# Splitting a convolution chunk between accumulating DMAs and VectorE, and preparing projection weights two tiles ahead, in a two-layer conv / attention / expert trunk

## The chip, the cores and the metric

The kernel runs on one core of one Trainium2 chip. The metric is the device time of one execution in microseconds (us); the median of the runs is given. The core's engines work side by side, each through its own queue in program order: TensorE (PE, matmuls; its weight loads are listed as PEld), VectorE (DVE), ScalarE (ACT), GpSimd (POOL) and SyncE (SP). DMAs are issued from the SP, ACT and POOL queues.

## The reference, cut to what matters

Two layers, each a mixer block and then an expert lookup, over 16 meta tokens and 256 tokens of width 1024. The change lies in the mixer:

```python
h = _rmsnorm(x, mix_g); z = h @ w_in          # conv_in, c_q, c_kv, k_rope, gate_logits
u = conv_in[..., :512] * sigmoid(conv_in[..., 512:])
u = _causal_depthwise_conv(u, conv_w, conv_b)  # 31 taps for each of 512 channels
u = silu(_layernorm(u, conv_ln_g, conv_ln_b)); y_conv = u @ w_conv_out
q = (_rmsnorm(c_q, q_a_g) @ w_uq); kv = (_rmsnorm(c_kv, kv_a_g) @ w_ukv)   # 8 heads
y_mla = chunk_causal_attention(q, k, v) @ w_mla_out
gates = sigmoid(gate_logits)
merged = gates[..., :1024] * y_conv + gates[..., 1024:] * y_mla
x = x + merged @ w_out
```

Then `_peer` picks 128 of 16384 experts for each token, and adds their outputs to `x`.

## The kernel before, in words

Everything is float32, channels on the 128 partitions and the T = 272 tokens along the free dimension (layer 1 computes only the last 256 in most places). The order of the instructions on each engine is written out by hand: Python generators (`attention`, `conv2`, `layernorm`) are advanced a step at a time between the matmul tiles, and whatever a step issues goes to the queues there.

**Weights.** `next_w` hands out weight tiles of 128 x 1024 from a ring of four 1 MB buffers `wraw`, which SP loads (line 85); `peek_w(n)` looks n tiles ahead.

**The gate loop.** `ztile` makes one 128-channel tile of `z` by eight matmuls. After eight tiles for the conv input (`upad`, four chunks of 128 channels) come 16 gate tiles, `for i in range(16)`. In each, DVE scales the tile (`g`, line 791), `next(att)` twice runs two pieces of the attention, and `taps(n, m)` does n conv taps on DVE and m steps of `conv2` on ACT and POOL. The attention's ACT pieces are the exponentials (`pr`, line 475), their scaling (line 485), and the copies `t` of the transposed probabilities (lines 505 to 507), which PE then multiplies by the values.

**The conv.** `conv` does the taps of chunks 1, 2 and 3 on DVE, one instruction each (`acc`, lines 623 and 625): 93 a layer, in portions given by the table `TAPS`. `conv2` does chunk 0: ACT multiplies the shifted input by a tap's weight, three taps into `part` and then three at a time into `cp` (line 635, two buffers in turn), and after each three POOL issues a DMA that adds `cp` to `part` (line 639, `accum_op`). Each such DMA has to wait for the one before it, since all add to `part`; and ACT may write a `cp` buffer only when the DMA that read it has ended. At the end two DVE adds sum `part` into `acc` (lines 642 and 643).

**The layernorm** begins when all taps are done: sums over the channels by PE (line 699), `acc` less the mean, squares, sums again, an inverse root in steps (lines 174 to 179), the product with it (line 719), on ACT a sigmoid and a scaled copy for each chunk (lines 722 and 723), the product of both (line 727), and at last its split in a high and a low part `uk` (lines 728 and 730), the source of the conv projection.

**The projections.** Weights go through PE as two parts: `high(i, n)` copies a weight tile to a rounded type on ACT (line 665), `low(i)` subtracts that from the tile on DVE (line 675), and `three` multiplies high by high, low by high and high by low. Tile i's parts lie in `wuq` (i = 0, 3, 6 ...), in `seln` and `upad` (1, 4, 7 ...), in `kh` (2), or in `acc` and `sqa` (5, 8 ...). `half_tile(0..3)` multiplies the attention's output by `w_mla_out` (source `sq`), `half_tile(4..7)` the conv's by `w_conv_out` (source `uk`), each followed by its merge with the gates on DVE.

Of the kernel before, what the change touches and what calls it, by code (L numbers as in the profile page):

```python
# [12 lines left out]
AF = mybir.ActivationFunctionType  # L13
OP = mybir.AluOpType
# [6 lines left out]
T = 272  # L21
NH = 8
KW = 31
EPS = 1e-6
NEG = -3.0e38
WS = 16384.0
TAPS = [3, 3, 6, 6] + [8] * 12
SCALE = 96 ** -0.5
NC_ = 58
GROUPS = ((64, 32), (64, 32))  # L30
# [18 lines left out]
def trunk_kernel(ctx: ExitStack, tc: tile.TileContext, a: dict, out: bass.AP, dbg=None, stop=None):  # L49
    nc = tc.nc  # L50
    V, S, G, PE = nc.vector, nc.scalar, nc.gpsimd, nc.tensor
# [37 lines left out]
    def peek_w(n):  # L89

        k = state["use"] + n
        return raws[k // 2][:, k % 2]

    def next_w():
        k = state["use"]
        state["use"] += 1
        if k % 2 == 0:
            if k // 2 in ring:
                dma_to(ring.index(k // 2) + RAW)
            state["w"] = raws[k // 2][:, 0]  # L100
            return state["w"]
        state["w"] = raws.pop(k // 2)[:, 1]
        return state["w"]
# [57 lines left out]
    def run_all(g):  # L161
        for _ in g:
            pass
# [18 lines left out]
    def dump(name, ap):  # L182
        if dbg is not None and name in dbg:
            nc.sync.dma_start(dbg[name], ap)
# [11 lines left out]
    for l in range(NL):  # L196
        last = l == NL - 1
        t0 = META if last else 0
# [38 lines left out]
        qh, kh = pp.tile([128, 8, T], F32, name="xh"), mp.tile([128, 8, T], F32, name="kh")  # L237
# [3 lines left out]
        upad = mp.tile([128, 4, T + KW - 1], F32, name="upad")  # L241
# [32 lines left out]
        def ztile(c0, x=None):  # L274
            x = xg if x is None else x
            n = T - c0
            w_ = next_w()
            p = zp.tile([128, 512], F32, name="z", bufs=3)
            for c in range(8):
                mm(p[:, :n], w_[:, c * 128:(c + 1) * 128], x[:, c, c0:], c == 0, c == 7)  # L280
            return p[:, :n]
# [20 lines left out]
        def aps():  # L302
            return ap_.tile([128, 512], F32, name="aps", bufs=5)

        cq = mp.tile([128, 3, T], F32, name="cq")
# [297 lines left out]
        acc = mp.tile([128, 4, T], F32, name="acc")  # L603

        def weight(c, k):
            return cl[:, C_CW + c * KW + k:C_CW + c * KW + k + 1]

        def bias(c):
            return cl[:, C_CB + c:C_CB + c + 1]

        ck = {1: 0, 2: 0, 3: 0}

        def conv(n, cs=(1, 2, 3)):

            for _ in range(n):
                c = min(cs, key=lambda c_: (ck[c_], c_))
                k = ck[c]
                if k == KW:
                    return
                ck[c] += 1  # L620
                u_ = upad[:, c, k + t0:k + T]
                if k == 0:
                    V.tensor_scalar(acc[:, c, t0:], u_, weight(c, k), bias(c), op0=OP.mult, op1=OP.add)
                else:
                    V.scalar_tensor_tensor(acc[:, c, t0:], u_, weight(c, k), acc[:, c, t0:], op0=OP.mult, op1=OP.add)  # L625

        part = mp.tile([128, 3, T], F32, name="part")

        def conv2():

            for k in range(0, KW, 3):
                u_ = mp.tile([128, 3, T], F32, name="cp", bufs=2) if k else part
                n = min(3, KW - k)
                for x in range(n):
                    S.activation(u_[:, x, t0:], upad[:, 0, k + x + t0:k + x + T], AF.Copy if k + x else AF.Identity,  # L635
                                 scale=weight(0, k + x), bias=0.0 if k + x else bias(0))
                    yield
                if k:
                    G.dma_start(part[:, 0:n, t0:], u_[:, 0:n, t0:], accum_op=OP.add)  # L639
            for _ in range(4):  # L640
                yield
            V.tensor_add(acc[:, 0, t0:], part[:, 0, t0:], part[:, 1, t0:])
            V.tensor_add(acc[:, 0, t0:], acc[:, 0, t0:], part[:, 2, t0:])
            yield

        parts = {}
# [1 line left out]
        def high(i, n):  # L648

            w_ = peek_w(n)  # L650
            x = {19: 3, 21: 4, 23: 1, 25: 2}.get(i, i % 3)
            if x == 0:
                t_ = mp.tile([128, 2, 1024], F32, name="wuq")
                hi, lo = t_[:, 0], t_[:, 1]
            elif x == 1:
                hi = mp.tile([128, 1024], F32, name="seln")
                lo = mp.tile([128, 1208], F32, name="upad")[:, 0:1024]
            elif i == 2 or x > 2:
                t_ = mp.tile([128, 8 * T], F32, name="kh" if x < 4 else "sq", tag="kh" if x < 4 else "sq")
                hi, lo = t_[:, 0:1024], t_[:, 1024:2048]  # L660
            else:
                hi = mp.tile([128, 4 * T], F32, name="acc")[:, 0:1024]
                lo = mp.tile([128, 4 * T], F32, name="sqa")[:, 0:1024]
            parts[i] = hi.bitcast(F32R), lo.bitcast(F32R), w_
            S.activation(parts[i][0], w_, AF.Copy)
            if i > 20:
                S.activation(parts[i][1], w_, AF.Copy, scale=-1.0)

        def low(i):

            hi, lo, w_ = parts[i]
            if i > 20:
                G.dma_start(lo, w_, accum_op=OP.add)
            else:
                V.tensor_tensor(lo, w_, hi.bitcast(F32), op=OP.subtract)

        def three(i, p, xs, wc, cs, first, end):

            hi, lo, _ = parts[i]
            for c in cs:  # L680
                s_ = slice((wc + c) * 128, (wc + c + 1) * 128)
                mm(p, hi[:, s_], xs[0][:, c, t0:], c == first, False)
                mm(p, lo[:, s_], xs[0][:, c, t0:], False, False)
                mm(p, hi[:, s_], xs[1][:, c, t0:], False, c == end)

        def half_tile(i, src):

            next_w()
            ps = []
            for f in range(2):  # L690
                p = (aps() if f else zp.tile([128, 512], F32, name="z", bufs=3))[:, :TQ]
                three(i, p, (src[:, 0], src[:, 1]), 4 * f, range(4), 0, 3)
                ps.append(p)
            return ps
# [48 lines left out]
        rs = vt["rs"]  # L743
# [8 lines left out]
        V.tensor_add(zkr[64:128], zkr[64:128], zk2[64:128])  # L752
        att = attention()
        cvp = conv2()

        def taps(n, m, cs=(1, 2, 3)):
            conv(n, cs)
            for _ in range(m):
                next(cvp, None)
# [20 lines left out]
        ln = None  # L780
        ng = [0]

        def gates(n):
            while ng[0] < n:
                g_ = gt[ng[0] // 8][:, ng[0] % 8, t0:]
                S.activation(g_, g_, AF.Sigmoid)
                ng[0] += 1

        for i in range(16):
            z = ztile(t0)  # L790
            V.tensor_mul(gt[i // 8][:, i % 8, t0:], z, rs[:, t0:])
            if ln is None:
                next(att, None)
                taps(TAPS[i] // 2, 2)
                next(att, None)
                taps(TAPS[i] - TAPS[i] // 2, 1)
                if min(ck.values()) == KW and next(cvp, "end") == "end":
                    ln = layernorm()
            else:
                next(ln, None)  # L800
                next(att, None)
                next(ln, None)
                next(att, None)
            if "exp" in vt:
                gates(min(i + 1, ng[0] + 2))
            if i == 14:
                high(0, 1)
                low(0)
        gates(16)
        run_all(att)  # L810
        conv(93)
        run_all(cvp)
        if ln is None:
            ln = layernorm()
        oo = vt["o"]
        dump("acc", acc)
        dump("rs", rs)
        dump("cq", cq)
        dump("qh", qh)
        dump("kh", kh)  # L820
        dump("oo", oo)
        high(1, 1)
        low(1)
        for i in range(4):
            ps = half_tile(i, oo)
            next(ln, None)
            next(ln, None)
            if i < 3:
                high(i + 2, 1)
            for f in range(2):  # L830
                V.tensor_mul(gt[1][:, 2 * i + f, t0:], gt[1][:, 2 * i + f, t0:], ps[f])
            if i < 3:
                low(i + 2)
        run_all(ln)
        high(5, 1)
        low(5)
        uu = vt["u"]

        xh = pp.tile([128, 8, T], F32, name="xh").bitcast(F32R)
# [236 lines left out]
        for i in range(16):  # L1076
# [9 lines left out]
            if i % 3 == 1:  # L1086
                k = next(ahead, None)
# [15 lines left out]
            if i == 1:  # L1103
                rs = rstd(st[:, :TQ], D, TQ, "m")
# [16 lines left out]
            if 4 <= i < 12:  # L1121
                c = i - 4
# [429 lines left out]
```

## Time and profile before

| what | before |
|---|---|
| median of 3 runs | 1747.59 us (1747.16 to 1747.74) |
| the profiled execution's own time | 1748.93 us |
| its span, first to last instruction | 1746.9 us |
| mean granted TensorE clock | 0.988 |
| PE busy | 1703.2 us (97%) |
| PE weight loads busy | 1608.4 us (92%) |
| DVE busy | 1139.8 us (65%) |
| ACT busy | 568.6 us (33%) |
| POOL busy | 312.8 us (18%) |

Times in a trace are counted from the span's start. Layer 0's gate loop runs from about 72 to 155 us, layer 1's from about 950 to 1039 us. A row of a timeline gives the start, the length, the engine, the line, the operation, what it writes and reads, how many instructions are merged in it, and in square brackets how long the engine had been idle before it and what ended that. A row of waits gives the total in us, the number of waits and the longest. Busy shares are means over stages of quite different kinds, so the argument goes by stage.

### The profile page before, as it was taken

The page shows a single profiled execution, that of the slowest core. Times are in us where ns is not written, and L with a number is a line of the kernel's source. Part 1 is how long each engine was busy: PE and PEld are TensorE (multiplying, and loading weights), DVE is VectorE, ACT ScalarE, POOL GpSimd, SP SyncE. Part 2 cuts the span into 40 slices and gives each one's busy share as a digit, 9 for nine tenths or more (in the row PEclk, how much of TensorE's full clock was granted, in tenths as well). Part 3 has the DMA queues.
Part 4 walks back from the last instruction along what each step waited for, and adds up shares of the span by engine and source line. Part 5 has one row for each costly group of instructions (what it writes and reads, how often), then busy time and mean ns, then how long its engine had stood idle before and what let it go on. Part 6 is the DMA issues. An engine that isn't in the chain of part 4 may idle for free.

```text
span 1746.9 us, 30498 instructions
## 1 busy us (share of the span) xinstructions
PE 1703.2 (97%) x11995; PEld 1608.4 (92%) x11995; DVE 1139.8 (65%) x2965; ACT 568.6 (33%) x1616; POOL 312.8 (18%) x360
## 2 busy tenths in 40 slices
PE   9998999999999999999999889999999999999998
PEld 7677999999999999999986679999999999999998
DVE  6686888897888544444456568897878885333332
ACT  3454633435454111000024546433354441000000
POOL 0010022222112223222200100212121112222220
PEclk9998999999999999999999899999999999999999
DMA  6363686999999999999953636869999999999995
GB/s 236 116 167 110 228 266 247 371 386 421 419 420 420 419 421 421 416 421 417 417 205 96 142 112 219 279 273 370 394 412 424 423 415 417 396 384 384 395 396 204
DMA packets 87152, 571.20 MB, mean 327 GB/s; under 512 B 9689, under 2 KB 16409, under 8 KB 19545
## 3 DMA queue, kind: packets, MB, share of 16 engines
q1 hardware_dynamic: 49488, 338.54, 49.4%
q0 software_dynamic: 36800, 230.11, 34.5%
q8 instruction: 94, 1.54, 0.3%
q10 hardware_dynamic: 720, 0.60, 0.1%
q14 instruction: 50, 0.40, 0.1%
HBM read 556.18 MB, written 1.05 MB: 319 GB/s over the span
## 4 chain that ended last, share of the span: by engine, by line
PE 57%; DMA 15%; DVE 12%; issue 10%; POOL 3%; ACT 2%; SPq 0%; POOLq 0%; DVEq 0%; ACTq 0%
PE po L57 26%; PE z L57 16%; PE A L57 9%; DMA wraw<-vn 7%; DMA gb<-uv,iww 6%; PE aps L57 4%; POOL gb L1318 3%; DMA part<-cp 2%; DVE va L1329 2%; DVE gb L1343 1%; PE wp L57 1%; DVE ex L1034 1%; PE sc L57 1%; PE xp L57 0%; DVE si L926 0%
## 5 line engine op out<-in xcount | busy, mean ns | idle before, releaser
L57 PE MATMUL A<-xh,wraw 128*128 128x160 f32 x3776 | 535.7, 301 | 1.2 <-ACT idxT L948 1.2
L57 PEld LDWEIGHTS A<-xh,wraw 128*128 128x128 f32 x3776 | 518.8, 191 | 1.6 <-issue 1.6
L1343 DVE SCALAR_TENSOR_TENSOR gb<-gb,xr 128x1024 f32<-128x1024 f32 x208 | 254.6, 1224 | 397.6 <-DMA gb<-uv,iww 395.3
L1318 POOL DMA_INDIRECT gb<-uv,iww x208 | 228.2, 1097 | 527.7 <-DVE va L1329 378.2
L57 PE MATMUL po<-Xh,wraw 128*128 128x160 f32 x2080 | 286.9, 300 | 2.8 <-DMA wraw<-vn 1.9
L57 PEld LDWEIGHTS po<-Xh,wraw 128*128 128x128 f32 x2080 | 283.1, 190 | 5.5 <-DMA wraw<-vn 4.2
L57 PE MATMUL po<-X,wraw 128*128 128x160 f32 x2016 | 279.5, 301 | 5.3 <-ACT gl L1378 2.9
L57 PEld LDWEIGHTS po<-X,wraw 128*128 128x128 f32 x2016 | 276.0, 191 | 8.3 <-DMA wraw<-vn 4.8
L57 PE MATMUL z<-xg,wraw 128*128 128x272 f32 (+2 forms) x1152 | 271.3, 393 | 0.3 <-DMA wraw<-w_in 0.3
L1329 DVE SCALAR_TENSOR_TENSOR va<-gb,am,va 128x1024 f32<-128x1024 f32 x203 | 259.9, 1280 | 0.6 <-ACT am L1354 0.4
L57 PEld LDWEIGHTS z<-xg,wraw 128*128 128x128 f32 (+1 forms) x1152 | 212.8, 190 | 47.8 <-issue 8.3
L1353 ACT ACTIVATE am<-am 128x1 f32<-128x1 f32 x208 | 41.3, 198 | 590.4 <-DVE gb L1343 590.3
L1257 ACT ACTIVATE ohA<-ohE,wlo 128x128 f16<-128x128 f16 x320 | 105.2, 429 | 7.4 <-DVE ohE L1254 6.7
L1317 POOL COPY warm<-wraw 1x1 f32<-1x1 f32 x86 | 34.7, 403 | 321.2 <-DMA wraw<-vn 321.0
L625 DVE SCALAR_TENSOR_TENSOR acc<-upad,cols,acc 128x272 f32<-128x272 f32 (+1 forms) x180 | 76.8, 485 | 0.2
L639 POOL DMA_DIRECT2D part<-cp x20 | 21.4, 1068 | 253.4 <-ACT cp L635 182.8
L1268 ACT ACTIVATE Xh<-wp 128x260 f32<-128x260 f32 (+18 forms) x80 | 25.0, 312 | 125.8 <-DVE Xh L1265 106.9
L1354 ACT ACTIVATE am<-am,iww 128x1 f32<-128x1 f32 x208 | 61.3, 295 | 6.8
L1254 DVE TENSOR_TENSOR ohE<-ioh,idxT 128x512 f16<-128x512 f16 x160 | 60.3, 419 | 0.0
L57 PE MATMUL wp<-ohE,ohA 128*128 128x128 f16 x640 | 51.7, 219 | 2.2 <-DVE ohA L1255 2.2
L57 PEld LDWEIGHTS <-ohA 128*128 128x128 f16 x640 | 43.2, 97 | 7.7 <-DVE ohA L1255 2.8
L57 PE MATMUL A<-xh,we 128*128 128x160 f32 x320 | 45.3, 299 | 0.0
(402 smaller groups left out, 1766.1 us busy)
## 6 DMA issues: line engine op xcount, KB each, us to landing
wraw<-vn SPq DMA_DIRECT2D x128, 1024.0 KB
wraw<-u SPq DMA_DIRECT2D x118, 1024.0 KB
wraw<-w_in SPq DMA_DIRECT2D x27, 1024.0 KB
wraw<-wq SPq DMA_DIRECT2D x16, 1024.0 KB
we<-u SPq DMA_DIRECT2D x10, 1024.0 KB
wraw<-w_out SPq DMA_DIRECT2D x8, 1024.0 KB
wraw<-w_mla SPq DMA_DIRECT2D x4, 1024.0 KB
wraw<-w_conv SPq DMA_DIRECT2D x4, 1024.0 KB
```

The source lines that it names most:

```text
L57: PE.matmul(o, l, r, start=start, stop=stop, skip_group_check=True)
L625: V.scalar_tensor_tensor(acc[:, c, t0:], u_, weight(c, k), acc[:, c, t0:], op0=OP.mult, op1=OP.add)
L639: G.dma_start(part[:, 0:n, t0:], u_[:, 0:n, t0:], accum_op=OP.add)
L1254: V.tensor_tensor(E[q], ioh[:, None].to_broadcast(full), pairs(q, b), op=OP.is_equal)
L1257: S.activation(A_[1][:, t // 2, :, t % 2], E[0][:, t // 2, :, t % 2], AF.Copy, scale=wlo[:, 4 * b + t:4 * b + t + 1])
L1268: S.activation(x_, p[:, :, a:b].rearrange("p t j -> p j t"), AF.Copy, scale=1.0 / WS)
L1317: G.tensor_copy(warm[0:1], state["w"][0:1, 0:1])
L1318: G.indirect_dma_start(out=g_, out_offset=None, in_=a[f"uv{l}"], in_offset=bass.IndirectOffsetOnAxis(ap=iww[i].bitcast(I32)[:, m // 16, 0, ...
L1329: V.scalar_tensor_tensor(vac[i], r, m_, vac[i], op0=OP.mult, op1=OP.add)
L1343: V.scalar_tensor_tensor(u_, u_, 1.0, xrs[i], op0=OP.mult, op1=OP.mult, accum_out=m_)
L1353: S.activation(m_, m_, AF.Gelu_apprx_tanh)
L1354: S.activation(m_, m_, AF.Copy, scale=iww[i][:, m // 16, 1, m % 16:m % 16 + 1])
```

## The change

Two edits, the same in both layers.

1. **The conv's chunk 0.** `conv2` now does taps 0 to 20 only (`KD` = 21): seven groups of three, so six accumulating DMAs in place of ten. It is advanced one or two steps a tile instead of three. Taps 21 to 30 of chunk 0 go to DVE, with the bias in the first of them, and the table `TAPS` is one higher a tile. At the end three DVE adds put `part` into `acc`, after the last taps.
2. **The projections' weight parts.** `high` and `low` of tile 2 are issued ahead of `half_tile(0)`, and in the loop those of tile i + 3 come right behind `half_tile(i)`, above the layernorm's step and the gate products. Before, tile i + 2 came there, its high part below the layernorm's steps and its low part below the products.

```diff
-TAPS = [3, 3, 6, 6] + [8] * 12
+TAPS = [4, 4, 7, 7] + [9] * 12
+KD = 21
...
-        ck = {1: 0, 2: 0, 3: 0}
-        def conv(n, cs=(1, 2, 3)):
+        ck = {1: 0, 2: 0, 3: 0, 0: KD}
+        def conv(n, cs=(0, 1, 2, 3)):
...
-                if k == 0:
+                if k == (0 if c else KD):
...
-            for k in range(0, KW, 3):
+            for k in range(0, KD, 3):
                 u_ = mp.tile([128, 3, T], F32, name="cp", bufs=2) if k else part
...
-            for _ in range(4):
+            for _ in range(2):
                 yield
-            V.tensor_add(acc[:, 0, t0:], part[:, 0, t0:], part[:, 1, t0:])
-            V.tensor_add(acc[:, 0, t0:], acc[:, 0, t0:], part[:, 2, t0:])
+            while ck[0] == KD:
+                yield
+            for x in range(3):
+                V.tensor_add(acc[:, 0, t0:], acc[:, 0, t0:], part[:, x, t0:])
...
-                taps(TAPS[i] // 2, 2)
+                taps(TAPS[i] // 2, 1)
                 next(att, None)
-                taps(TAPS[i] - TAPS[i] // 2, 1)
+                taps(TAPS[i] - TAPS[i] // 2, i % 2)
...
         gates(16)
+        high(1, 1)
         run_all(att)
...
-        high(1, 1)
         low(1)
+        high(2, 2)
+        low(2)
         for i in range(4):
             ps = half_tile(i, oo)
+            if i == 2:
+                run_all(ln)
+            if i < 3:
+                high(i + 3, 2)
+                low(i + 3)
             next(ln, None)
-            next(ln, None)
-            if i < 3:
-                high(i + 2, 1)
             for f in range(2):
                 V.tensor_mul(gt[1][:, 2 * i + f, t0:], gt[1][:, 2 * i + f, t0:], ps[f])
-            if i < 3:
-                low(i + 2)
+            next(ln, None)
         run_all(ln)
-        high(5, 1)
-        low(5)
```

PE's and SP's rows stand in the same order as before, and POOL has three plain rows fewer a layer and one short one fewer. What moves is on ACT and DVE. First ACT in layer 1's gate loop, around the second set of exponentials (`cp` are the conv steps, `pr` the exponentials and their scaling, `t` the copies for the attention's next matmuls). Before:

```order
L635 ACTIVATE cp<-upad,cols_62 128x256 x3
L475 ACTIVATE pr_7813,sm<-aps,nb,sc 128x144
L475 ACTIVATE pr_7814,sm<-aps,nb,sc 128x272
L475 ACTIVATE pr_7813,sm<-aps,nb,sc 128x144
L475 ACTIVATE pr_7814,sm<-aps,nb,sc 128x272
L635 ACTIVATE cp<-upad,cols_62 128x256 x3
L505 ACTIVATE t_7861<-aps 128x512
L506 ACTIVATE t_7862<-aps 128x256
L507 ACTIVATE t_7863<-aps 16x512
```

After:

```order
L635 ACTIVATE cp<-upad,cols_62 128x256
L476 ACTIVATE pr_7799,sm<-aps,nb,sc 128x144
L476 ACTIVATE pr_7800,sm<-aps,nb,sc 128x272
L476 ACTIVATE pr_7799,sm<-aps,nb,sc 128x144
L476 ACTIVATE pr_7800,sm<-aps,nb,sc 128x272
L635 ACTIVATE cp<-upad,cols_62 128x256 x2
L506 ACTIVATE t_7847<-aps 128x512
L507 ACTIVATE t_7848<-aps 128x256
L508 ACTIVATE t_7849<-aps 16x512
```

Three conv steps stood between one tile's exponentials and the copies `t`; now two do, and one instead of three ahead of the exponentials.

Second, ACT behind the gate loop in layer 0: the layernorm's last sigmoid and scaled copy, the last six gate sigmoids, and the weight parts (`seln` is tile 1's high part, `kh` tile 2's, `wuq` tile 3's). Before:

```order
L722 ACTIVATE sqa<-acc,cols_61 128x272
L723 ACTIVATE acc<-acc,cols_61 128x272
L786 ACTIVATE g_596<-g_596 128x272 x6
L665 ACTIVATE seln<-wraw 128x1024
L728 ACTIVATE uk<-acc 128x272 x4
L665 ACTIVATE kh<-wraw 128x1024
L665 ACTIVATE wuq<-wraw 128x1024
```

After:

```order
L723 ACTIVATE sqa<-acc,cols_61 128x272
L724 ACTIVATE acc<-acc,cols_61 128x272
L787 ACTIVATE g_596<-g_596 128x272 x6
L666 ACTIVATE seln<-wraw 128x1024
L666 ACTIVATE kh<-wraw 128x1024
L666 ACTIVATE wuq<-wraw 128x1024
L729 ACTIVATE uk<-acc 128x272 x4
```

Tiles 2 and 3 moved ahead of the layernorm's `uk`; tile 1 stands where it stood, behind the gate sigmoids.

More of the change, by code (lines that the diff above doesn't have):

```diff
@@ L629, in conv2 @@
         def conv2():
-            for k in range(0, KW, 3):
+            for k in range(0, KD, 3):
                 u_ = mp.tile([128, 3, T], F32, name="cp", bufs=2) if k else part
[L633 to L636, printed above, removed]
+                for x in range(3):
+                    S.activation(u_[:, x, t0:], upad[:, 0, k + x + t0:k + x + T], AF.Copy, scale=weight(0, k + x))
                     yield
                 if k:
-                    G.dma_start(part[:, 0:n, t0:], u_[:, 0:n, t0:], accum_op=OP.add)
-            for _ in range(4):
+                    G.dma_start(part[:, :, t0:], u_[:, :, t0:], accum_op=OP.add)
+            for _ in range(2):
                 yield
-            V.tensor_add(acc[:, 0, t0:], part[:, 0, t0:], part[:, 1, t0:])
-            V.tensor_add(acc[:, 0, t0:], acc[:, 0, t0:], part[:, 2, t0:])
+            while ck[0] == KD:
+                yield
+            for x in range(3):
+                V.tensor_add(acc[:, 0, t0:], acc[:, 0, t0:], part[:, x, t0:])
             yield
@@ L754, in trunk_kernel, with taps @@
         cvp = conv2()
-        def taps(n, m, cs=(1, 2, 3)):
+        def taps(n, m, cs=(0, 1, 2, 3)):
             conv(n, cs)
@@ L815, in trunk_kernel @@
         oo = vt["o"]
[L816 to L821, printed above, removed]
-        high(1, 1)
         low(1)
+        high(2, 2)
+        low(2)
         for i in range(4):
             ps = half_tile(i, oo)
+            if i == 2:
[3 more added lines that the diff above has]
+                low(i + 3)
             next(ln, None)
-            next(ln, None)
-            if i < 3:
-                high(i + 2, 1)
             for f in range(2):
                 V.tensor_mul(gt[1][:, 2 * i + f, t0:], gt[1][:, 2 * i + f, t0:], ps[f])
-            if i < 3:
-                low(i + 2)
+            next(ln, None)
         run_all(ln)
-        high(5, 1)
-        low(5)
         uu = vt["u"]
```

## The prediction

> **What bounds the kernel.** I read the page's chain by line first, to see who sets the end; then PE's waits in the mixer of each layer; then the chain in order of time and the timelines at each wait that the change touches.
>
> ```profile
> PE po L57 26%; PE z L57 16%; PE A L57 9%; DMA wraw<-vn 7%; DMA gb<-uv,iww 6%; PE aps L57 4%; POOL gb L1318 3%; DMA part<-cp 2%; DVE va L1329 2%; DVE gb L1343 1%; PE wp L57 1%; DVE ex L1034 1%; PE sc L57 1%; PE xp L57 0%; DVE si L926 0%
> ```
>
> PE holds most of the chain. The conv's accumulating DMA, `part<-cp`, holds 2%, though it should run beside the matmuls. PE's waits in layer 1's mixer (900 to 1090 us: total, times, longest):
>
> ```profile
> PE aps L57 <- ACT t L505: 5.7, 1, 5.7
> PE z L57 <- ACT seln L665: 5.2, 1, 5.2
> PE aps L57 <- ACT pr L475: 1.7, 1, 1.7
> ```
>
> In layer 0 only the wait for `seln` appears among those over 1 us. So two places matter: a stall in layer 1's gate loop (`t` and `pr`), and one at the projections in both layers (`seln`). The chain in order of time at the first:
>
> ```profile
> 951.31 4.68 DMA part<-cp
> ...
> 956.54 8.78 DMA part<-cp
> ...
> 965.86 9.63 DMA part<-cp
> ...
> 976.01 7.69 DMA part<-cp
> ...
> 983.79 0.91 ACT cp L635 x2
> 984.69 0.49 ACT t L505
> ...
> 985.23 2.59 PE aps L57 x12
> ```
>
> Four accumulates in a row make 30.8 us of the chain and take up to 9.63 us each, one in each tile. ACT has two `cp` buffers, so it must wait for a DMA, and `t` stands behind it in its queue. ACT's waits for this DMA, layer 1's row first, then layer 0's:
>
> ```profile
> ACT cp L635 <- DMA part<-cp: 20.1, 6, 7.4
> ACT cp L635 <- DMA part<-cp: 6.1, 5, 3.5
> ```
>
> Layer 0's 6.1 us never reach PE. What layer 1's cost, from PE's timeline, three rows at the stall and then the same three groups undisturbed:
>
> ```profile
> 977.53 1.98 PE L57 MATMUL aps<-kh,xh 98*128 98x144 f32 x8 [1.67 <-ACT pr L475]
> 985.23 2.59 PE L57 MATMUL aps<-t,vt 128*64 128x256 f32 x12 [5.71 <-ACT t L505]
> 987.75 6.41 PE L57 MATMUL z<-xg,wraw 128*128 128x256 f32 x16
> ...
> 998.54 1.57 PE L57 MATMUL aps<-kh,xh 98*128 98x144 f32 x8
> 1000.04 1.45 PE L57 MATMUL aps<-t,vt 128*64 128x256 f32 x12
> 1001.42 3.72 PE L57 MATMUL z<-xg,wraw 128*128 128x256 f32 x16
> ```
>
> Idle: 1.67 + 5.71 = 7.38 us. Slower matmuls: (1.98 - 1.57) + (2.59 - 1.45) + (6.41 - 3.72) = 4.24 us. The reason stands in the granted clock (PEclk, third column from the end, in stretches of 5 us and then one of two tiles):
>
> ```profile
> 980.00:985.00 5.00, 0.00 (x0) 0.00 (x0) 2.18 (x6) 1.21 (x3) 0.76 (x1) 0.50 0.60 111
> 985.00:990.00 5.00, 4.77 (x17) 2.90 (x18) 0.00 (x0) 3.88 (x11) 1.19 (x2) 0.50 0.53 79
> 990.00:995.00 5.00, 5.00 (x22) 4.09 (x21) 4.10 (x13) 3.18 (x12) 0.90 (x2) 0.68 0.53 79
> 995.00:1000.00 5.00, 5.00 (x27) 4.19 (x24) 4.10 (x13) 3.90 (x11) 1.14 (x2) 1.00 0.62 92
> ...
> 994.20:1005.20 11.00, 11.00 (x65) 8.91 (x63) 8.86 (x25) 6.82 (x20) 2.53 (x2) 1.00 0.75 167
> ```
>
> The clock falls to half in the wait and stays there for some 8 us after. The stall costs 7.38 + 4.24 = 11.6 us.
>
> The Trainium skill (TensorE: Matmul & The Clock Gate, "What's actually happening") says that an idle window of about 3.4 us halves the clock and a busy one of that length restores it. By it, as an estimate, the slower matmuls would be worth 3.4 / 2 = 1.7 us and the stall 9.1 us. The trace agrees on the halving and disagrees on the recovery, so the rows decide.
>
> **The conv's edit, part by part.** *Fewer accumulates.* Six come in place of ten, and one in two tiles. Even the slowest, 9.63 us, fits into the 11.0 us of two tiles (the last row above), and with two buffers ACT has a further group's time. I take the whole stall as gone: -11.6 us. Ends: 0 if the DMAs become so much later that ACT still waits, -11.6 if not; nearest is the full gain, since in layer 0 a DMA every 5 to 6 us already keeps ACT's wait off PE. In layer 0 there is no wait of PE to take away: 0.
>
> *ACT* loses ten products a layer; it is not late but for the DMA: 0.
>
> *DVE* gains ten taps and one add a layer. From layer 1's timeline:
>
> ```profile
> 1015.26 0.43 DVE L642 TENSOR_TENSOR acc<-part 128x256 f32<-128x256 f32 x1 [1.61 <-DMA part<-cp]
> ...
> 1016.39 3.25 DVE L625 SCALAR_TENSOR_TENSOR acc<-upad,cols,acc 128x256 f32<-128x256 f32 x8
> ...
> 1021.80 1.27 DVE L625 SCALAR_TENSOR_TENSOR acc<-upad,cols,acc 128x256 f32<-128x256 f32 x3
> 1024.34 0.42 DVE L791 TENSOR_TENSOR g<-z,rq_ym 128x256 f32<-128x256 f32 x1 [1.26 <-PE z L57]
> ```
>
> A tap is 3.25 / 8 = 0.40 us, so 10 x 0.40 + 0.43 = 4.4 us a layer. Two more taps in two tiles make 8.86 (DVE's busy time, the third, in the stretch of two tiles above) + 0.8 = 9.7 of 11.0 us: hidden under PE, with 1.3 us to spare. If that cover were gone, 4.4 us a layer would show.
>
> *The end of the conv.* The adds of `part` now stand behind the last taps, ahead of the layernorm's sums, so PE would wait for what is late. Here three taps end at 1023.07 and DVE then idles 1.26 us. Two taps and three adds take 2 x 0.40 + 3 x 0.43 = 2.1 instead of 1.27 us, 0.8 us more, which fits by 0.4 us; the tap more in the tile before is paid by the wait of 1.61 us at 1015.26, which is no longer there. The last accumulate is issued about 1.5 tiles ahead of the adds, some 8 us; at 4 to 5 us it is in time, at 9.63 it holds DVE for up to 2 us. I take 0, ends 0 and +2 us a layer, nearest to 0 because by then the four slow transfers are past.
>
> The Trainium skill (SBUF — State Buffer, "SBUF: two separate sides") warns that a DMA issued from GpSimd waits for its descriptors while certain DVE instructions run; whether a tap is one of them it does not say. If so, more taps would lengthen each accumulate, by 9/8, 9.63 to 10.8 us as an estimate, still inside 11.0, so its sum is the same with no margin left. The rows speak against it: the transfer of 976.01 took 7.69 us with DVE nearly idle, and the one before this row took 1.26 + 3.86 us in the stretch where DVE was busy 8.86 of 11.0:
>
> ```profile
> 999.81 1.27 POOL L639 DMA_DIRECT2D part<-cp  x1 [3.86 <-DMA part<-cp]
> ```
>
> **The weights' edit.** The stall it stands beside, PE, then ACT, then PE and DVE behind it:
>
> ```profile
> 163.28 0.59 PE L57 MATMUL z<-sq,seln 128*128 128x272 f32 x1 [5.22 <-ACT seln L665]
> ...
> 155.65 0.62 ACT L722 ACTIVATE sqa<-acc,cols 128x272 f32<-128x272 f32 x1 [9.04 <-DVE acc L719]
> ...
> 160.28 2.01 ACT L786 ACTIVATE g<-g 128x272 f32<-128x272 f32 x6
> 162.19 1.04 ACT L665 ACTIVATE seln<-wraw 128x1024 fp32r<-128x1024 f32 x1
> ...
> 1049.56 1.43 DVE L730 TENSOR_TENSOR uk<-acc,uk 128x256 fp32r<-128x256 f32 x4
> ...
> 1051.57 1.22 DVE L675 TENSOR_TENSOR kh<-wraw,kh 128x1024 fp32r<-128x1024 f32 x1
> ...
> 1058.47 0.28 PE L57 MATMUL z<-uk,seln 128*128 128x256 f32 x1
> ...
> 1076.54 0.39 PE L57 MATMUL z<-xh,upad 128*128 128x256 f32 x1 [0.43 <-DVE upad L675]
> ```
>
> PE waits 5.22 us for tile 1's high part, which is behind eight layernorm pieces and six sigmoids (155.65 to 162.2). In the new order `seln` still stands behind all of these. Only tiles 2, 3 and later move, and PE waits for none of them. So this stall stays in both layers: 0. What moves can be gained back at one place, the 0.43 us at 1076.54, and there ACT's next copy waits for PE's tile again; I take -0.1, ends 0 and -0.4 a layer.
>
> The cost: tiles 2 and 3 (two ACT copies of 1.04, two DVE differences of 1.22) now stand ahead of the layernorm's last step, and tile 3's copy waits for `half_tile(0)` to leave `wuq`. That is over before the sigmoids end, so the wait is nothing. `uk` ends 2.4 us later, in layer 1 at 1050.99 + 2.4 = 1053.4; PE wants it at 1058.47. The gate products behind it are 2.4 us later too, and free their PSUM buffers before the fourth tile: 0.
>
> **Sum.** -11.6 - 0.1 = -11.7 us against the profiled execution's 1748.93 (span 1746.9, 2.0 outside it): 1737.2. The median is 1.34 us below that execution: 1735.9, so 1736. Nothing behind layer 1's mixer depends on absolute time, so I shift the rest rigidly.
>
> **Rivals.** A change below 0.2% (3.5 us) I count as the same.
> - *Part of the stall stays* (10%). The accumulates run against weight loads, and the third `cp` group still comes before the slow ones are over. A wait of 3 to 6 us left gives 1739 to 1742. For it: 9.63 is near 11.0. Against: two buffers.
> - *DVE becomes the bound* (7%). 4.4 us show in each layer: 1736 + 8.8 = 1744.8, within the bound. For it: 9.7 of 11.0 us. Against: 1.3 us free in two tiles.
> - *The stall only moves* (5%). The DMAs stay as late because the weight loads hold them, and DVE waits at the new adds instead of ACT at `cp`: about 1747.5. Against: layer 0.
> - *Slower* (4%): the layernorm's last step, behind tile 3's copy, reaches PE late. At 1058.47 there are 5.1 us to spare. If `uk` came 10 us later still, PE would wait 4.9 us and lose about 4.2 us to the halved clock, in both layers 18 us: 1754. It is slower than before by 0.2% from about 8.5 us later on. Against: nothing there is that long.
> - *The stall for `seln` goes as well* (2%): twice 5.22 and the clock's 4 us, so 1718. Against: the order.
>
> The rest, 72%, is the forecast, 1733.5 to 1738.5. To leave out no more than 2 in 10 the range takes in the partial stall: 1732.5 to 1742. Faster 0.84, same 0.12, slower 0.04.
>
> **What the profile after would show.** Right: no wait of PE for `t` or `pr` in layer 1's gate loop, granted clock 1.00 there, ACT's wait for the DMA near 0, `part<-cp` gone from the chain; six accumulates a layer; DVE busy about 9.7 of 11 us in two tiles; the 5.2 us for `seln` still there in both layers with half clock behind it. Wrong: a wait of PE for `acc` at the layernorm's sums, for `uk` at the fifth half tile, or DVE waiting for `part` at the new adds by more than 2 us; or a gate loop in layer 0 longer than before.

## The result, and the profile after

The changed kernel takes 1735.17 us (median of 4 runs, 1733.18 to 1736.42) against 1747.38 us before (median of 4 runs): a ratio of 0.9928, 95% interval 0.9913 to 0.9943, 12.2 us less. The prediction was 1736 us. The profiled execution took 1733.18 us (span 1731.4), the lowest of the four; so the two traces differ by 15.5 us of span where the medians differ by 12.2.

The chain by line, after:

```profile
PE po L58 27%; PE z L58 20%; PE A L58 20%; DMA wraw<-vn 6%; PE aps L58 4%; DMA gb<-uv,iww 2%; POOL gb L1314 2%; PE wp L58 1%; PE sc L58 1%; PE xp L58 0%; DVE gb L1339 0%; DVE va L1325 0%; DVE upad L676 0%; DVE rq_w L179 0%; DVE rq_w L178 0%
```

`part<-cp` has left it. PE's waits in layer 1's mixer, 900 to 1090 us; here as in all rows of after, lines from 28 to about 810 are one higher than in the kernel before:

```profile
PE z L58 <- ACT seln L666: 5.2, 1, 5.2
PE z L58 <- DVE upad L676: 1.1, 2, 0.7
PE z L58 <- DVE wuq L676: 0.7, 1, 0.7
```

The waits for `pr` and `t` are gone; the one for `seln` stands as it was. PE's timeline at the place of the old stall, and the layernorm's sums that end the conv:

```profile
974.92 1.57 PE L58 MATMUL aps<-kh,xh 98*128 98x144 f32 x8
976.42 1.45 PE L58 MATMUL aps<-t,vt 128*64 128x256 f32 x12
977.80 3.72 PE L58 MATMUL z<-xg,wraw 128*128 128x256 f32 x16
...
1011.50 1.89 PE L58 MATMUL aps<-acc,ones 128*128 128x256 f32 x8
```

The three groups that took 1.98, 2.59 and 6.41 us take 1.57, 1.45 and 3.72. The same sums started at 1024.13 before:

```profile
1024.13 1.89 PE L57 MATMUL aps<-acc,ones 128*128 128x256 f32 x8
```

That is 12.63 us earlier. Layer 1's first projection already started 0.79 us earlier (884.94 instead of 885.73), so the conv stage itself gained 11.84 us. Granted clock and DVE, first in 5 us and then in two tiles (times after the stretch: its length, then PE, PE's weight loads, DVE, ACT, POOL; third from the end PEclk):

```profile
980.00:985.00 5.00, 5.00 (x30) 4.41 (x29) 5.00 (x15) 4.88 (x16) 1.27 (x1) 1.00 0.04 7
...
982.62:993.62 11.00, 11.00 (x63) 8.91 (x63) 9.60 (x28) 6.37 (x21) 1.27 (x1) 1.00 0.52 133
```

DVE is busy 9.60 of 11.0 us and PE, busy throughout, waits for nothing there; the clock is full. The time from issue to landing stands in the trace for two of layer 1's six accumulates, those issued at 950.53 and 999.56:

```profile
DMA to landing us min/median/max: 4.6/4.6/4.7
```

For the other four the packets tell it: the last packet of each of the six goes 4.2 to 4.5 us after its issue, that of the two above at 4.4 and 4.3.

### The profile page after: what moved, and what is told of

It reads as the page before. It is cut to its first block, busy times and chain, and to the rows that moved or that the text cites. A ratio compares the mean times of both kernels' runs of the same rounds, so it can differ in the third digit from the quotient of the medians.

```text
span 1731.4 us, 30489 instructions
## 1 busy us (share of the span) xinstructions
PE 1694.2 (98%) x11995; PEld 1603.0 (93%) x11995; DVE 1148.1 (66%) x2987; ACT 559.4 (32%) x1596; POOL 306.5 (18%) x352
## 4 chain that ended last, share of the span: by engine, by line
PE 75%; issue 9%; DMA 8%; DVE 4%; POOL 2%; ACT 2%; POOLq 0%; SPq 0%; ACTq 0%; DVEq 0%
PE po L58 27%; PE z L58 20%; PE A L58 20%; DMA wraw<-vn 6%; PE aps L58 4%; DMA gb<-uv,iww 2%; POOL gb L1314 2%; PE wp L58 1%; PE sc L58 1%; PE xp L58 0%; DVE gb L1339 0%; DVE va L1325 0%; DVE upad L676 0%; DVE rq_w L179 0%; DVE rq_w L178 0%
## 5 line engine op out<-in xcount | busy, mean ns | idle before, releaser
L1314 POOL DMA_INDIRECT gb<-uv,iww x208 | 223.7, 1076 | 526.5 <-DVE va L1325 377.0
L1313 POOL COPY warm<-wraw 1x1 f32<-1x1 f32 x86 | 40.7, 473 | 320.8 <-DMA wraw<-vn 320.8
L626 DVE SCALAR_TENSOR_TENSOR acc<-upad,cols,acc 128x272 f32<-128x272 f32 (+1 forms) x198 | 84.2, 484 | 0.2
L638 POOL DMA_DIRECT2D part<-cp x12 | 13.2, 1102 | 249.4 <-ACT cp L635 249.4
```

Source lines behind the costliest of these rows:

```text
L638: G.dma_start(part[:, :, t0:], u_[:, :, t0:], accum_op=OP.add)
L1313: G.tensor_copy(warm[0:1], state["w"][0:1, 0:1])
L1314: G.indirect_dma_start(out=g_, out_offset=None, in_=a[f"uv{l}"], in_offset=bass.IndirectOffsetOnAxis(ap=iww[i].bitcast(I32)[:, m // 16, 0, ...
```

## Why the accumulates were slow before

The rows that answer this stand in two queues. Here are SP's weight loads of 1 MB in the kernel before; the accumulates of the chain in the prediction were issued at 956.54, 965.86 and 976.01:

```profile
957.31 0.33 SPq L85 DMA_DIRECT2D wraw<-w_in  x1
...
966.49 0.33 SPq L85 DMA_DIRECT2D wraw<-w_in  x1
...
975.90 0.33 SPq L85 DMA_DIRECT2D wraw<-w_in  x1
```

Each slow one (8.78, 9.63, 7.69 us) was issued within 0.8 us of a load; the first of the chain, at 951.31, 2.4 us behind the load of 948.96, took 4.68. What happens beside a load, the packets of the two queues show (number, MB, share of the 16 DMA engines; q1 carries SP's loads, q0 POOL's accumulates). First the kernel before from 956.54, the issue of the first slow accumulate, to 962.1; then the changed kernel from 982.94, an issue clear of the loads, to 987.05:

```profile
q1 hardware_dynamic: 121, 0.99, 68.2%
...
q0 software_dynamic: 387, 0.39, 63.2%
```

In the first stretch only the load moved; the accumulate's first packet went at 962.15, 5.6 us after its issue. The other two slow ones sent theirs after 5.6 and 4.3 us, those clear of a load after 1.8 to 2.0 us. A slow accumulate is thus mostly one that starts late, while the load's packets go.

Once late, an accumulate starts the next one late, and that meets the next load. After the change an accumulate falls between two loads:

```profile
975.12 0.33 SPq L86 DMA_DIRECT2D wraw<-w_in  x1
...
982.94 1.27 POOL L638 DMA_DIRECT2D part<-cp  x1 [10.17 <-ACT cp L635]
...
986.10 0.33 SPq L86 DMA_DIRECT2D wraw<-w_in  x1
```

## The experiments

### Which of the two edits: each alone

The conv's edit alone (the changed kernel, its projection loop put back):

```diff
-        high(2, 2)
-        low(2)
...
-            if i < 3:
-                high(i + 3, 2)
-                low(i + 3)
+                high(i + 2, 1)      # below the layernorm's steps
...
+                low(i + 2)          # below the gate products
```

> The changed kernel with the weights' tiles put back where they were before (one tile ahead, below the layernorm's steps); the conv's edit stays. Theory (the conv's edit carries the gain; the weights' edit alone gave 1745.5 against 1747.6 us, 0.07%, within its interval): no wait of PE for t or pr in layer 1, 1735 to 1737 us. Rival (the weights' edit is worth 1 us a layer): 1737 to 1738 us, with the 0.43 us waits back and a later end of the half clock behind the seln stall.

1733.8 us, ratio 0.9928 (0.9914 to 0.9941): all of the gain. The weights' edit alone (the same lines the other way round, on the kernel before):

> The kernel before with the weights' edit alone (tiles 2 and 3 ahead of the layernorm's last step), the conv left at 31 taps by ten accumulates. Theory (the whole gain is the conv's): layer 1's gate loop keeps its stall, PE waits about 1.7 us for pr and 5.7 us for t, and the time is the kernel before's less 0.1, 1747.2 us. Rival (the weights' edit brings the earlier end of the half clock behind the seln stall, 0.65 us in layer 0's profile and as much in layer 1): 1745.5 us or less, with the half clock ending sooner behind that stall in both layers.

1745.47 us against 1747.58, ratio 0.9993 (0.9984 to 1.0002). The stall is still there:

```profile
PE aps L57 <- ACT t L505: 3.9, 1, 3.9
PE aps L57 <- ACT pr L475: 2.1, 1, 2.1
```

The median fell on the rival's number, the rival's mark did not come: the half clock behind layer 0's `seln` stall lasted 10.2 us, as in the kernel before, and in the run of the conv's edit alone 10.2 us too. The weights' edit is worth 0.16% at most and perhaps nothing; these runs cannot tell the predicted 0.1 us from 0.

### How often, or how many

The changed kernel with its six accumulates one in each tile:

```diff
-                taps(TAPS[i] // 2, 1)
+                taps(TAPS[i] // 2, 2)
...
-                taps(TAPS[i] - TAPS[i] // 2, i % 2)
+                taps(TAPS[i] - TAPS[i] // 2, 1)
```

> The changed kernel with its six accumulates issued one in each tile as before, instead of one in two tiles (21 taps by DMA, 10 more on DVE, the weights' edit kept). Theory (what matters is how often they come: two accumulates and a weight load in two tiles do not fit into their 11 us): the first four are as slow as before, ACT waits for a cp buffer at the fifth group again, and PE's stall in the gate loop comes back with 5 to 11 us: 1741 to 1747 us. Rival (what matters is their number, four fewer): the time stays at the changed kernel's, 1735 us.

1746.17 us, ratio 0.9994 (0.9985 to 1.0002): the whole gain is lost. PE's waits, then ACT's:

```profile
PE aps L58 <- ACT t L506: 4.2, 1, 4.2
PE aps L58 <- ACT pr L476: 2.1, 1, 2.1
...
ACT cp L635 <- DMA part<-cp: 16.9, 4, 7.8
```

It is the pace that counts: 21 taps by DMA instead of 31 alone bring nothing. With the pace, ACT's old order came back too, three `cp` steps between the exponentials and `t`; that this order alone does not make the stall is shown by the one-run kernel below, which has it and in its faster profile waits for neither `pr` nor `t`.

### A buffer more

The kernel before with three `cp` buffers in layer 1:

```diff
-                u_ = mp.tile([128, 3, T], F32, name="cp", bufs=2) if k else part
+                u_ = mp.tile([128, 3, T], F32, name="cp", bufs=3 if last else 2) if k else part
```

> The kernel before with a third buffer for cp in layer 1, all ten accumulates kept, one in each tile. Theory A (ACT lacks a buffer; what is late is only made late by two buffers): the four slow accumulates take 30.8 us where four tiles take 22, 8.8 us too long; a third buffer is worth a tile, 5.5 us, and later accumulates catch up: PE idles 0 to 2 us instead of 7.4, about 1736 to 1739 us. Rival B (POOL issues an accumulate only when the last has landed, and the chain of ten, 64 us from 951.3 to 1015.3 in the profile before, is longer than the tiles it should hide under): the stall leaves the gate loop and comes back as DVE's wait for part at the adds and PE's wait for the layernorm's sums, 8 to 12 us: 1744 to 1748 us.

1753.73 us, ratio 1.0039 (1.0025 to 1.0053): slower than before. Waits of PE, then of DVE:

```profile
PE aps L57 <- DVE acc L643: 6.5, 1, 6.5
PE aps L57 <- DVE acc L625: 4.9, 1, 4.9
PE aps L497 <- DVE sq L530: 3.9, 2, 2.8
...
DVE acc L642 <- DMA part<-cp: 15.5, 1, 15.5
```

Rival B holds, and more than it said. The ten accumulates wait for each other, and a buffer does not shorten that row. The buffer took the delay off `t`, PE reached the end of the conv sooner, and there, in a profiled execution of 1757.33 us, DVE waited 15.5 us for `part`, in front of the layernorm's sums and of its own remaining taps (`acc L625`). Two late accumulates at the end, in POOL's timeline:

```profile
1003.95 1.27 POOL L639 DMA_DIRECT2D part<-cp  x1 [4.91 <-DMA part<-cp]
1013.15 1.27 POOL L639 DMA_DIRECT2D part<-cp  x1 [7.93 <-DMA part<-cp]
1021.98 0.90 POOL L639 DMA_DIRECT2D part<-cp  x1 [7.56 <-DMA part<-cp]
```

Loads were issued at 1004.56 and 1014.23, beside the first two of these. The forecast of 1744 to 1748 was 6 us short: it took the row of accumulates as long as before, 64 us, while it met three loads more and took 73.

### One run a partition instead of three

The kernel before with layer 1's `cp` and `part` whole, so that an accumulate moves one run of 3264 bytes a partition:

```diff
-                    S.activation(u_[:, x, t0:], upad[:, 0, k + x + t0:k + x + T], ...
+                    S.activation(u_[:, x], upad[:, 0, k + x:k + x + T], ...
...
-                    G.dma_start(part[:, 0:n, t0:], u_[:, 0:n, t0:], accum_op=OP.add)
+                    G.dma_start(part[:, 0:n], u_[:, 0:n], accum_op=OP.add)
```

> The kernel before with cp and part in layer 1 written from column 0 instead of column 16, so that each accumulate moves one run of 3264 bytes a partition, as in layer 0, instead of three of 1024; 6% more bytes. Theory (the three short runs make layer 1's accumulates slow, up to 9.63 us where layer 0's come every 5 to 6 us): POOL's issue falls from 1.26 to 0.85 us, ACT's wait for them from 20 to about 6 us as in layer 0, PE's stall is gone, 1736 us. Rival (the weight loads beside them make them slow, whatever their shape): the accumulates still take 8 to 9 us in the same place and PE's stall stays, 1746 to 1748 us.

1739.70 us, ratio 0.9956 (0.9940 to 0.9971), but its times lie in two groups, 1733.8 to 1737.3 and 1742.1 to 1746.7 us. The profiled execution, 1735.33 us, shows no wait for `t` or `pr`, an issue of 0.85 us, and

```profile
ACT cp L635 <- DMA part<-cp: 9.5, 5, 3.5
```

in place of 20.1 us. The same kernel once more, for the upper group:

> The kernel before with one-run accumulates in layer 1 once more, for the two groups of its times (1733.8 to 1737.3 and 1742.1 to 1746.7 us). If the profiled execution falls into the upper group: theory (an accumulate in each tile now and then still starts beside a weight load, and is then late for its buffer): PE waits for t or pr in layer 1's gate loop by 3 to 6 us at a halved clock, and two or more accumulates in a row take over 6 us. Rival (the 7 us lie elsewhere, behind the mixers): no wait in the gate loop, later starts in the expert stages. If it falls into the lower group: no wait in the gate loop, as in the first profile.

This time the profiled execution, 1742.39 us, belongs to the upper group (the three runs: 1737.61, 1737.88, 1742.39). PE's wait in layer 1, and the accumulates and loads around it:

```profile
PE aps L497 <- DVE sq L530: 4.7, 2, 3.0
```

```profile
976.35 0.85 POOL L639 DMA_DIRECT2D part<-cp  x1 [5.88 <-DMA part<-cp]
984.44 0.85 POOL L639 DMA_DIRECT2D part<-cp  x1 [7.24 <-DMA part<-cp]
989.85 0.85 POOL L639 DMA_DIRECT2D part<-cp  x1 [4.55 <-ACT cp L635]
998.64 0.85 POOL L639 DMA_DIRECT2D part<-cp  x1 [7.94 <-DMA part<-cp]
...
976.96 0.33 SPq L85 DMA_DIRECT2D wraw<-w_in  x1
...
989.80 0.33 SPq L85 DMA_DIRECT2D wraw<-w_in  x1
```

The theory holds in place and size; only the wait has another name (`sq`, which stands behind ACT's late `cp`). Two accumulates in a row take over 6 us: the one before these rows, issued at 969.62, 2.1 us behind a load, takes 0.85 + 5.88 = 6.7 us, and that of 976.35, 0.6 us ahead of a load, 0.85 + 7.24 = 8.1 us. The one at 984.44 takes 5.4 or less, and that of 989.85, issued on a load, 8.8 us. So both rivals of the first run had a part: with one run the accumulates are shorter and mostly keep clear of the loads, and where one meets a load it is as slow as with three.

### The other tile

The changed kernel with each accumulate one tile away:

```diff
-                taps(TAPS[i] - TAPS[i] // 2, i % 2)
+                taps(TAPS[i] - TAPS[i] // 2, 1 - i % 2)
```

> The changed kernel with the pairs and singles of cp exchanged between even and odd tiles, so that each accumulate is issued one tile, 5.5 us, away from its place now. In the changed kernel the accumulates of layer 1's steady part are issued about 8 us behind a weight load and 3 us ahead of the next (982.94 between 975.12 and 986.10) and land in 4.6 us; in the kernel before the slow ones were issued within 0.9 us of a load (956.54 and 957.31, 965.86 and 966.49, 976.01 and 975.90). Now they come about 2 us behind a load. Theory (a load beside it lengthens an accumulate, but one in two tiles has 11 us and two buffers): they take 5 to 9 us, no PE wait in the gate loop, 1734 to 1737 us. Rival (the changed kernel gains only because its accumulates fall between the loads): ACT waits for cp again and PE for t or pr, 1738 to 1747 us.

1734.10 us, ratio 0.9928 (0.9915 to 0.9941). The accumulates now came closer to the loads than forecast, 0.2 to 0.9 us behind them (966.29, 975.00, 986.40 and 997.39 against 965.37, 974.78, 985.76 and 996.75), and still neither ACT nor PE waited for one. Their packets show that they were slower there: the last packet of these four goes 6.0 to 7.2 us after the issue, that of the one at 955.43, 0.8 us ahead of a load, 8.9 us, against 4.2 to 4.5 us in the changed kernel. So the gain does not hang on where the accumulates fall, but on the 9 to 11 us that each of these five has.

### How much DVE can take

12 and then 3 taps by DMA instead of 21, each tile's taps one and two higher so that the conv ends in the same tile:

```diff
-TAPS = [4, 4, 7, 7] + [9] * 12
-KD = 21
+TAPS = [5, 5, 8, 8] + [10] * 12        # second run: [6, 6, 9, 9] + [11] * 12
+KD = 12                                # second run: 3, no accumulate at all
```

> The changed kernel with 12 of the 31 taps by accumulating DMA instead of 21: three accumulates a layer, nine more taps on DVE, the tiles' numbers of taps raised by one so that the conv ends in the same tile. Theory (DVE's taps hide under PE as long as two tiles' work is below 11.0 us: 9.6 now, 10.4 then): the same time, 1734 to 1737 us. Rival (DVE is in effect the bound already, since PE waits for it tile by tile): 9 x 0.40 = 3.6 us show in each layer, 1742 us, with PE's waits for mx, nb or acc in the gate loops.

1734.35 us, ratio 0.9928 (0.9915 to 0.9942): nine more taps a layer cost nothing that the times show. Two stretches of two tiles:

```profile
971.50:982.50 11.00, 11.00 (x63) 8.89 (x62) 9.98 (x28) 4.76 (x15) 0.00 (x0) 1.00 0.52 131
982.50:993.50 11.00, 11.00 (x64) 8.91 (x63) 10.96 (x32) 5.27 (x16) 0.00 (x0) 1.00 0.28 97
```

> The changed kernel with 3 of the 31 taps on ACT and none by DMA: no accumulate at all, 18 more taps a layer on DVE, the tiles' numbers of taps raised by two so that the conv ends in the same tile. DVE's work in two tiles is then about 9.6 + 4 x 0.40 = 11.2 us of 11.0 (with 12 taps by DMA it was 9.98 and 10.96 in two pairs of tiles, and the time the same). Theory (DVE becomes the bound only where its work passes the tiles' length): 0.2 to 1 us in each of five pairs of tiles, 1 to 4 us a layer, 1737 to 1743 us, with PE waiting for nb, g or acc in the gate loops. Rival (there is still slack at the loop's ends that takes it up): 1734 to 1736 us.

1738.31 us, ratio 0.9939 (0.9923 to 0.9954; 1734.57 to 1741.51): about 3 us above the changed kernel's 1735.2. The two intervals overlap, so the times alone do not prove a loss; the trace shows where one arises. In the same stretch, and PE's new wait in layer 1:

```profile
971.50:982.50 11.00, 11.00 (x64) 8.87 (x62) 10.97 (x32) 4.88 (x15) 0.00 (x0) 1.00 0.36 132
```

```profile
PE aps L58 <- DVE kh L447: 0.7, 1, 0.7
```

DVE is full here and PE is just not held. What shows is at the loop's beginning, where `kh`, behind more taps, comes 0.7 us late in layer 1 and 0.6 in layer 0. The theory's number came out (1737 to 1743), its place did not: the trace shows one late product a layer, with one step of half clock behind layer 1's, not a loss in every pair of tiles. That makes 0.7 + 0.6 us and about 1.7 us for the half clock, 3 us together.

### The stall that stayed

The changed kernel with tile 1's high part right behind tile 0's, its low part a tile later:

```diff
             if i == 14:
                 high(0, 1)
+                high(1, 2)
                 low(0)
+            if i == 15:
+                low(1)
         gates(16)
-        high(1, 1)
...
-        low(1)
```

> The changed kernel with tile 1's high part (seln) copied right behind tile 0's, in the gate loop's fifteenth tile, while ACT waits for the layernorm, and its low part in the sixteenth; all else as changed. Theory (the 5.2 us stall in each layer is tile 1's copy standing behind eight layernorm pieces and six sigmoids): the wait for seln goes in both layers; tile 2's copy (kh), which still stands behind them, is late next, and PE waits about 2.2 us for it and 0.7 for its low part, 3 us less a layer than now, and the slower clock behind it shortens by 0 to 2.5 us: 1723 to 1729 us. Rival (the stall only moves to kh and keeps its length, since PE just comes to it sooner): 1733 to 1736 us.

1728.17 us, ratio 0.9891 (0.9876 to 0.9906). The stall has moved on by one tile and is shorter, layer 0:

```profile
163.04 0.39 PE L58 MATMUL z<-sq,kh 128*128 128x272 f32 x1 [2.20 <-ACT kh L666]
164.30 2.38 PE L58 MATMUL z<-sq,kh 128*128 128x272 f32 x11 [0.87 <-DVE kh L676]
```

So tile 2 goes ahead as well, and the last six sigmoids behind it:

```diff
                 high(1, 2)
+                high(2, 3)
...
             if i == 15:
                 low(1)
+                low(2)
-        gates(16)
...
-        high(2, 2)
-        low(2)
...
             ps = half_tile(i, oo)
-            if i == 2:
-                run_all(ln)
+            gates(10 + 2 * i)
+            for f in range(2):
+                V.tensor_mul(gt[1][:, 2 * i + f, t0:], gt[1][:, 2 * i + f, t0:], ps[f])
             if i < 3:
                 high(i + 3, 2)
                 low(i + 3)
-            next(ln, None)
-            for f in range(2):
-                V.tensor_mul(gt[1][:, 2 * i + f, t0:], gt[1][:, 2 * i + f, t0:], ps[f])
-            next(ln, None)
+            run_all(ln)
```

> As the run with seln early, and tile 2's high part (kh) copied there too, both low parts in the sixteenth tile, the last six sigmoids two by two behind the half tiles instead of ahead of them, and the gate products ahead of tile 3's copy. Theory: no tile of the four is late any more; 5.2 + 0.7 us of idle time and the half clock behind it (5.0 us in layer 0 and 3.7 in layer 1 of the changed kernel's profile, half of that lost) go, about 8 us a layer: 1718 to 1723 us. Rival (the layernorm's last step becomes late for the fifth half tile, since PE reaches it 8 us sooner): PE waits 3 to 5 us for uk in each layer and the clock falls there: 1725 to 1732 us.

1720.86 us, ratio 0.9855 (0.9840 to 0.9870). Of the waits for weight parts in layer 1 there remain

```profile
PE z L58 <- DVE upad L676: 1.4, 2, 1.0
PE z L58 <- DVE wuq L676: 1.3, 2, 0.7
```

and the clock stays at 1.00 from 150 to 175 us, where the changed kernel's was halved. `uk` was in time, against the rival. A last step moved two low parts further ahead on DVE:

```diff
-            if i == 14:
-                high(0, 1); high(1, 2); high(2, 3); low(0)
+            if i == 13:
+                high(0, 2); high(1, 3); high(2, 4); low(0)
...
+            if i == 1:
+                high(4, 2); low(4)          # ahead of the gate products
...
-            if i < 3:
+            if i in (0, 2):                 # high and low of tile i + 3, behind them
```

> As the run with three tiles early, and two low parts moved ahead on DVE: tile 0's (with the three copies) one gate tile sooner, into DVE's idle time between the steps of the layernorm's root, and tile 4's ahead of tile 1's gate products. Theory: the waits left there, 0.6 and 0.7 us in layer 0 and 1.3 and 1.0 in layer 1, go or halve: 2 to 3.5 us less, 1717.5 to 1719 us. Rival (the layernorm's last step becomes as much later and holds PE at uk instead): 1721 us or more, with a wait of PE for uk.

1719.68 us, ratio 0.9848 (0.9835 to 0.9862), 27.7 us below the kernel before and 15.5 below the changed one. The step itself brought 1.2 us by the medians, within both intervals and less than the 2 to 3.5 expected: the waits for low parts fell, and PE now waits for the gate products that were pushed back (`g`, 0.8 us in layer 0, 1.2 in layer 1).

## Why the prediction was right, point by point

- *The stall in layer 1's gate loop, -11.6 us.* Right in place and size: the stage gained 11.84 us in the trace, clock included. That the pace of the accumulates is the cause is shown by the run with six accumulates, one a tile (no gain), and that ACT's `cp` wait carries it by ACT's 20.1 us, which are gone after.
- *"With two buffers ACT has a further group's time".* As an argument it was weak: the run with three buffers shows that buffers do not help where the row of accumulates is too long. The argument that holds is the other one in the same step, that 9.63 us fit into 11.0.
- *What makes the accumulates slow.* The prediction left it open ("run against weight loads") and named layer 0 as the nearest row. The offsets from the loads and the two profiles of the one-run kernel bear it out: beside a load an accumulate takes about twice as long, and three short runs in place of one add some 0.4 us (5.1 to 5.2 against 4.5 to 4.9 us from one issue to the next where no load is near). That each slow one meets a load, and that its packets start late, is shown; why they mostly do not go between the load's packets, no run tells, and none took the loads away.
- *Layer 0: 0.* Layer 0's expert stage began 1.3 us earlier, which was not forecast. The half clock behind `seln` lasted one step of 3.4 us less there in this profile, worth 1.7 us; the run with the conv's edit alone has the longer one and the same gain, so I count it as chance.
- *DVE's 4.4 us a layer hidden.* Right: 9.60 of 11.0 us forecast as 9.7, and room for nine taps more, as the 12-tap run shows. The rival "DVE becomes the bound" had its point too low: only with 18 taps more does a trace show a product of DVE late in the gate loop, by 0.7 us.
- *The end of the conv, 0.* Right. The last three adds follow the taps without a wait, and DVE idles 0.65 us behind them:

```profile
1008.93 0.87 DVE L626 SCALAR_TENSOR_TENSOR acc<-upad,cols,acc 128x256 f32<-128x256 f32 x2
1009.72 1.34 DVE L644 TENSOR_TENSOR acc<-acc,part 128x256 f32<-128x256 f32 x3
1011.70 0.42 DVE L792 TENSOR_TENSOR g<-z,rq_ym 128x256 f32<-128x256 f32 x1 [0.65 <-PE z L58]
```

- *The descriptors' rule.* The Trainium skill (SBUF — State Buffer, "SBUF: two separate sides") warns that a DMA issued from GpSimd waits for its descriptors while certain DVE instructions run. If taps were among these, more taps would lengthen the accumulates. The one issued at 982.94 fell into a stretch with DVE busy 5.00 of 5.00 us, and its last packet went 4.3 us after the issue, as with the other five; taps of this form did not hold it up. One row that the prediction set against the rule was misread: in the 7.69 us of the transfer of 976.01 DVE was not nearly idle but busy for 3.65 us, though idle in the 1.27 us of POOL's issue.
- *The weights' edit, -0.1, and the `seln` stall kept.* Right as far as it can be told; the place named for the 0.1 us did not gain, for the wait of 0.43 us at 1076.54 is one of 0.44 us at 1063.41 after. `uk` ended 4.9 us before PE came to it, 1040.60 against 1045.52; the forecast's was 5.1:

```profile
1039.18 1.42 DVE L731 TENSOR_TENSOR uk<-acc,uk 128x256 fp32r<-128x256 f32 x4
...
1045.52 0.28 PE L58 MATMUL z<-uk,seln 128*128 128x256 f32 x1
```

- *The sum.* 1736 against 1735.17 us. The further 2 to 3 us in the two profiles lie in the expert stages, where PE's small waits differ from run to run (the kernel before ran from 1744.55 to 1752.37 us over all its runs here). That the times agree within 1 us is in part luck: the medians of the kernel before alone lie between 1746.64 and 1747.94 us, and one step of half clock more or less is worth 1.7 us.

## What to carry to other kernels

A row of DMAs that must follow each other is to be sized by its slowest members, here those that meet a weight load (7.7 to 9.6 us), and not by an undisturbed one (4.7 us): if two tiles' worth of them and the load do not fit into two tiles, a further buffer only moves the wait to the end, and here made it dearer. Issuing half as many per tile, with the work given to an engine whose stage has room, took it off the path here. And a wait that an edit stands beside is worth looking at for what stands ahead of it in the waiting queue: moving two copies into ACT's idle time and six sigmoids behind the half tiles took the time from 1735.2 to 1720.9 us, a larger gain than that of the change itself.

## What the runs showed of the hardware

The half clock comes in steps of about 3.4 us. In rows of 1 us, the first and last of the half-clock spell at the projections of layer 0, before (3.4 x 3), after (3.4 x 2) and with `seln` early (3.4 x 1); the rows left out between them are all 0.50:

```profile
160.00:161.00 1.00, 0.00 (x0) 0.00 (x0) 0.00 (x0) 1.00 (x4) 0.00 (x0) 0.69 0.00 0
...
170.00:171.00 1.00, 1.00 (x8) 1.00 (x8) 0.84 (x2) 0.79 (x1) 0.00 (x0) 0.69 0.00 0
```

```profile
161.00:162.00 1.00, 0.00 (x0) 0.00 (x0) 0.00 (x0) 1.00 (x5) 0.00 (x0) 0.71 0.00 0
...
168.00:169.00 1.00, 1.00 (x9) 1.00 (x8) 1.00 (x4) 0.35 (x1) 0.00 (x0) 0.88 0.99 410
```

```profile
164.00:165.00 1.00, 0.70 (x5) 0.70 (x6) 1.00 (x2) 0.00 (x0) 0.00 (x0) 0.95 0.00 0
...
168.00:169.00 1.00, 1.00 (x9) 1.00 (x8) 1.00 (x4) 0.97 (x2) 0.00 (x0) 0.84 1.06 451
```

A row of clock c spent 2(1 - c) us at half: 0.62 + 9 + 0.62 = 10.2, 0.58 + 6 + 0.24 = 6.8, and 0.10 + 3 + 0.32 = 3.4 us. The spell in the old gate-loop stall, counted likewise, was 13.65 us, four steps. This corrects the prediction's reading. It set "some 8 us" against the 3.4 us of the Trainium skill (TensorE: Matmul & The Clock Gate, "What's actually happening"); that page also says that the windows run freely and do not start anew with the kernel, and the whole steps agree with it: the same stall of 5.2 us cost three steps in one profile and two in another. What makes a step count as busy stays open. In the kernel before, one with PE busy for 2.8 of its 3.4 us brought the clock back in layer 1 (1047.7 to 1051.1) and not in layer 0 (163.8 to 167.2), and in the old gate-loop stall one with PE shown busy throughout (986.4 to 989.8) did not either. The trace does not bear out that a whole window must be idle: with `seln` early a wait of 2.20 us and one of 0.87 led to a step, and in the run with 3 taps by DMA a wait of 0.68 us in layer 1 did (0.30 + 3 + 0.10 = 3.4 us at half from 961 to 966), while the 0.71 us for `wuq` in the changed kernel did not. What decides there stays open, too.
